# Condition vectors written as rows in eight pieces, and other order of small loads, in a two-block transformer kernel

## Chip, cores and metric

The kernel runs on one core of a Trainium2 chip. The metric is the device time of one execution in microseconds (us). TensorE is PE in the profile, VectorE DVE, ScalarE ACT, GpSimd POOL and SyncE SP; SP's queue issues nearly all transfers.

## What is computed

One sequence of 256 tokens of width 1024 goes through two blocks of two layers each. Block a has in each layer a gated feed-forward part (ffn), a mixer (retention, stick-breaking attention, state space) and a second ffn; block b has a mixer (three attentions) and an ffn. Every part is normalised, scaled and shifted by vectors that come from a condition `c`, and its result is gated by another such vector. Cut to one part of block a:

```python
mod = (silu(c) @ ada_w[l] + ada_b[l]).reshape(B, 9, 1024)[:, None]
u = modulate(rmsnorm(h, norm_ffn1[l]), mod[:, :, 0], mod[:, :, 1])   # u * (1 + scale) + shift
h = h + 0.5 * (1.0 + mod[:, :, 2]) * swiglu(u, ffn1_wg[l], ffn1_wu[l], ffn1_wd[l])
...
u = modulate(rmsnorm(h, norm_mix[l]), mod[:, :, 3], mod[:, :, 4])
...
h = h + (1.0 + mod[:, :, 5]) * mixed
```

All of it is in float32. There are 32 condition vectors of 1024 elements, each the product of the condition with 1024 x 1024 weights.

## The kernel before

**Work and stages.** The program is ten phases in a row: ffn, mixer, ffn for each layer of block a, then mixer, ffn for each layer of block b. The tokens are two tiles of 128 rows, `h[0]` and `h[1]`, which stay in SBUF. Every float32 product is three matmuls (`mm3`): each operand is split into a rounded high part H and a rest L, and H.H, H.L and L.H are added. A weight tile of 128 x 1024 is loaded by SP (`dma_next`, L306), cast to H by ACT (`prep_H`, L321), and DVE forms L = raw - H (`prep_L`, through `tt`, L185). The raw tiles, H, L, the condition tiles and the gate rows share one pool `s` of 36 buffers.

**An ffn.** For each block j of 256 hidden columns PE makes gate and up (`A`), ACT takes the silu (`post`, through `act`, L206), DVE multiplies (`m<-m,A`, L185), PE transposes the product (`trans`, through `tr`, L182, `T<-ident,m`), ACT and DVE split it into H and L, and `down` multiplies it into the accumulators `B`. Near a phase's end `ffn` yields event 0: `run` calls `fin_a(0)`, which adds the gated accumulators to `h[0]`, sums the squares on ACT, takes the reciprocal root on POOL (`rstd2`, L227 and L229), and normalises on DVE (`ts`, L198). Event 2 lets `fin_b(0)` transpose and modulate it for the next phase; event 1 does the second token tile.

**The condition vectors.** `ada_gen` runs beside the phases. For a vector it loads eight tiles of 128 x 1024 (`ada_load`, L501), and DVE multiplies each with the condition and sums (`ada_dot`, L506), one every `PACE[phase]` units of the program's own clock; a tile is asked for one dot ahead. The result is `v`, 128 x 8. Twenty of the vectors are used in this form. Twelve are gates (kinds h, p, c) and are needed as one row of 1024 on all partitions: `ada_fin` adds the bias on DVE (`g<-v,vtab`), ACT writes `v` as a row to DRAM (L550, `row<-g`), and ACT reads it back onto 128 partitions (L554, `s<-row`).

**Order.** Each engine takes its instructions in order. That order is made when the program is built: the phases' generator is the main lane, `ada_gen`, `ada_fin` and the weights' preparation are side lanes that are stepped whenever the main lane has advanced by so many units (`yield 3.0`, `self.pump(...)`), and a scheduler then places the instructions by their dependences and buffers. A DMA inside `issue_after(last_dma)` stays behind the load before it in SP's queue; one outside of it may be placed earlier. `d_skip` (L1272, the mixer of block a) and two gains `gqg` (L1373, the mixer of block b, from which POOL makes tables, L1377 and L1381) are loaded outside of it.

## Times and profile of the kernel before

| What | Value |
| --- | --- |
| median of three runs | 1949.09 us (1947.65 to 1954.33) |
| the profiled execution | 1949.93 us |
| its span | 1948.2 us |
| its mean granted clock of PE | 0.992 |
| PE busy | 1888.2 us, 97%, 9228 matmuls and transposes |
| DVE busy | 1452.8 us, 75% |
| ACT busy | 991.4 us, 51% |
| POOL busy | 68.7 us, 4% |

The span is the time from the first to the last instruction that the profile has. A busy time is the time in which the engine had an instruction at work. A timeline row gives start, duration, engine, line, operation, what it writes and reads, how many like it follow each other, and in brackets how long the engine had been idle just before and which instruction released it.

### The profile page before, as it was taken

The page shows a single profiled execution, that of the slowest core. Times are in us where ns is not written, and L with a number is a line of the kernel's source. Part 1 is how long each engine was busy: PE and PEld are TensorE (multiplying, and loading weights), DVE is VectorE, ACT ScalarE, POOL GpSimd, SP SyncE. Part 2 cuts the span into 40 slices and gives each one's busy share as a digit, 9 for nine tenths or more (in the row PEclk, how much of TensorE's full clock was granted, in tenths as well). Part 3 has the DMA queues.
Part 4 walks back from the last instruction along what each step waited for, and adds up shares of the span by engine and source line. Part 5 has one row for each costly group of instructions (what it writes and reads, how often), then busy time and mean ns, then how long its engine had stood idle before and what let it go on. Part 6 is the DMA issues. An engine that isn't in the chain of part 4 may idle for free.

```text
span 1948.2 us, 25535 instructions
## 1 busy us (share of the span) xinstructions
PE 1888.2 (97%) x9228; PEld 1555.2 (80%) x9228; DVE 1452.8 (75%) x2242; ACT 991.4 (51%) x1649; POOL 68.7 (4%) x135
## 2 busy tenths in 40 slices
PE   7999899999999999999989989999999899999998
PEld 5888798888888788988878868778888687778886
DVE  7877788788878786787777767678878576788552
ACT  5634556554445444576644435744544357546541
POOL 0000000100000000001000012100000011000000
PEclk9999999999999999999999999999999899999999
DMA  9979675389877896864698766467889663676650
GB/s 371 355 293 369 222 293 184 125 260 360 283 281 276 277 356 222 282 207 133 205 280 298 244 180 171 142 207 273 281 337 302 183 170 122 231 255 231 226 164 22
DMA packets 151344, 471.18 MB, mean 242 GB/s; under 512 B 36657, under 2 KB 36785, under 8 KB 151090
## 3 DMA queue, kind: packets, MB, share of 16 engines
q1 hardware_dynamic: 137010, 463.21, 69.2%
q10 hardware_dynamic: 14208, 6.34, 1.3%
q8 instruction: 72, 1.18, 0.2%
q14 instruction: 54, 0.44, 0.1%
HBM read 468.40 MB, written 1.10 MB: 241 GB/s over the span
## 4 chain that ended last, share of the span: by engine, by line
PE 59%; issue 28%; DVE 6%; DMA 4%; ACT 2%; POOL 1%; SPq 0%; ACTq 0%; DVEq 0%; POOLq 0%
PE A L170 39%; PE B L170 17%; PE T L182 3%; DVE s L185 2%; DMA row<-g 2%; DMA s<-in_ada_w 1%; DVE m L185 1%; ACT m L206 1%; ACT s L321 1%; DMA s<-in_ffn_wd 1%; DVE s L506 1%; DMA s<-in_ffn_gu 1%; DVE s L203 1%; DVE sm L1696 0%; DVE h L185 0%
## 5 line engine op out<-in xcount | busy, mean ns | idle before, releaser
L170 PE MATMUL A<-s,uH 128*128 128x512 f32 (+1 forms) x2976 | 936.2, 395 | 4.5 <-ACT uH L214 2.4
L185 DVE TENSOR_TENSOR s<-s,s 128x1024 fp32r<-128x1024 f32 (+2 forms) x638 | 754.1, 1198 | 124.7 <-ACT s L321 119.1
L321 ACT CAST s<-s 128x1024 fp32r<-128x1024 f32 (+1 forms) x618 | 624.0, 1043 | 96.7 <-DVE s L185 32.9
L170 PEld LDWEIGHTS A<-s,uH 128*128 128x128 f32 x2976 | 550.2, 189 | 121.7 <-issue 9.3
L170 PE MATMUL A<-s,uL 128*128 128x512 f32 (+1 forms) x1488 | 581.5, 392 | 0.3 <-DVE uL L185 0.3
L170 PE MATMUL B<-s,m 128*128 128x512 f32 (+2 forms) x1696 | 405.6, 387 | 0.7 <-ACT m L214 0.5
L170 PEld LDWEIGHTS B<-s,m 128*128 128x128 f32 x1696 | 310.6, 189 | 61.7 <-ACT m L214 1.9
L506 DVE SCALAR_TENSOR_TENSOR s<-s,cb 128x1024 f32<-128x1024 f32 x256 | 311.3, 1218 | 50.1 <-DMA s<-in_ada_w 43.5
L170 PEld LDWEIGHTS A<-s,uL 128*128 128x128 f32 x1488 | 280.4, 188 | 60.1 <-DVE uL L185 2.6
L206 ACT ACTIVATE m<-A 128x256 f32<-128x256 f32 x126 | 48.2, 383 | 246.6 <-PE A L170 246.4
L214 ACT CAST m<-T 128x256 fp32r<-128x256 f32 x132 | 48.9, 372 | 218.8 <-PE T L182 207.1
L170 PE MATMUL A<-uH,s 128*128 128x256 f32 (+1 forms) x672 | 128.0, 287 | 2.4 <-ACT s L1429 2.3
L185 DVE TENSOR_TENSOR m<-m,A 128x256 f32<-128x256 f32 x126 | 52.5, 417 | 86.0 <-ACT m L206 85.2
L182 PE MATMUL T<-ident,m 128*128 128x128 f32 (+1 forms) x488 | 85.6, 276 | 29.9 <-DVE m L185 27.7
L182 PEld LDWEIGHTS T<-ident,m 128*128 128x128 f32 (+1 forms) x488 | 62.8, 139 | 58.9 <-DVE m L185 33.1
L170 PEld LDWEIGHTS A<-uH,s 128*128 128x128 f32 (+1 forms) x672 | 105.6, 188 | 4.1 <-ACT s L1429 2.8
L170 PE MATMUL B<-s,s 128*128 128x512 f32 (+3 forms) x432 | 103.2, 384 | 0.9 <-ACT s L206 0.5
L185 DVE TENSOR_TENSOR m<-T,m 128x256 fp32r<-128x256 f32 x132 | 55.1, 420 | 56.8 <-ACT m L214 56.5
L170 PE MATMUL A<-uL,s 128*128 128x256 f32 (+1 forms) x336 | 95.5, 284 | 0.0
L170 PEld LDWEIGHTS B<-s,s 128*128 128x128 f32 (+1 forms) x432 | 78.7, 188 | 16.6 <-DVE s L203 1.3
L206 ACT ACTIVATE m<-h 128x512 f32<-128x512 f32 x44 | 27.8, 632 | 83.6 <-DVE h L185 83.6
L170 PEld LDWEIGHTS A<-uL,s 128*128 128x128 f32 (+1 forms) x336 | 63.3, 188 | 0.7
(189 smaller groups left out, 1193.6 us busy)
## 6 DMA issues: line engine op xcount, KB each, us to landing
s<-in_ffn_gu SPq DMA_DIRECT2D x264, 512.0 KB, 5.8
s<-in_ada_w SPq DMA_DIRECT2D x240, 512.0 KB, 6.5
s<-in_w_in_blk SPq DMA_DIRECT2D x152, 512.0 KB, 5.1
s<-in_ffn_wd SPq DMA_DIRECT2D x88, 512.0 KB, 5.8
s<-in_ffn_w_down SPq DMA_DIRECT2D x44, 512.0 KB, 4.8
s<-in_w_out SPq DMA_DIRECT2D x40, 512.0 KB, 4.3
s<-in_final_ada_w SPq DMA_DIRECT2D x16, 512.0 KB, 8.7
s<-row ACTq DMA_DIRECT2D x12, 512.0 KB, 7.3
```

The costliest lines, as they stand in the source:

```text
L170: self.last = self.nc.tensor.matmul(out, l, r, start=start, stop=stop, skip_group_check=True)
L182: self.nc.tensor.transpose(out, in_, self.ident[:p, :p])
L185: self.nc.vector.tensor_tensor(o, x, y, op=op)
L203: self.nc.vector.scalar_tensor_tensor(o, x, s, y, op0=op0, op1=op1)
L206: return self.nc.scalar.activation(o, x, f, **kw)
L214: self.nc.scalar.copy(H, x)
L321: self.last_H = self.nc.scalar.copy(H[:, :n], raw[:, :n])
L506: self.nc.vector.scalar_tensor_tensor(raw, raw, 1.0, self.cb, op0=ALU.mult, op1=ALU.mult, accum_out=v)
```

## The change

The vector v is transposed on PE to 8 x 128, copied by DVE, and written to DRAM as eight rows of 128; write and read are issued by SP, each with its place in the queue of loads. Condition tiles are asked for two dots ahead. The normalisation of the first token tile at the end of an ffn is put behind the last product (`post(j, 1)`, new event 3). The loads of `d_skip`, `gqg` and the constants keep their place in SP's queue (`queue`). Four of the ten paces differ. Lines below L405 move by up to 13.

```diff
--- before.py
+++ after.py
@@ -91,7 +91,7 @@
     return t.astype(np.float32)
 
 
-PACE = (3.2, 2.8, 4.1, 3.8, 3.6, 4.8, 4.8, 3.9, 5.0, 3.0)
+PACE = (3.9, 2.6, 4.1, 3.8, 3.6, 4.4, 3.6, 3.9, 5.0, 3.0)
 
 
 class Lane:
@@ -402,7 +402,7 @@
             evac(half, ps[:, :].rearrange("p (c n) -> p c n", c=2))
 
 
-    def fin_a(self, tt, accs, gate, extra=None):
+    def fin_a(self, tt, accs, gate, extra=None, lazy=False):
 
         h = self.h[tt]
         sq = self.m2([128, 512])
@@ -423,11 +423,15 @@
         r = self.rstd2(ss)
         if extra is not None:
             r = extra(tt, r)
-        xn = self.m4([128, 1024])
-        for nb in range(2):
-            c = slice(nb * 512, nb * 512 + 512)
-            self.ts(xn[:, c], h[:, c], r, ALU.mult)
-        return xn
+
+        def norm():
+            xn = self.m4([128, 1024])
+            for nb in range(2):
+                c = slice(nb * 512, nb * 512 + 512)
+                self.ts(xn[:, c], h[:, c], r, ALU.mult)
+            return xn
+
+        return norm if lazy else norm()
 
     def new_u(self):
         return (self.t([128, 2, 8, 128], "uH", 1, F32R), self.t([128, 2, 8, 128], "uL", 1, F32R))
@@ -496,6 +500,11 @@
         self.nc.sync.dma_start(self.cb, bass.AP(src.tensor, src.offset, [[0, 128], [1, 1024]]))
         self.act(self.cb, self.cb, AF.Silu)
 
+    def queue(self, out, in_):
+
+        with self.tc.issue_after(self.last_dma.ins):
+            self.last_dma = self.nc.sync.dma_start(out, in_)
+
     def ada_load(self, w, ft):
         raw = self.m4([128, 1024])
         self.nc.sync.dma_start(raw, w[ft * 128:ft * 128 + 128, :])
@@ -515,7 +524,8 @@
             ld.append(self.ada_load(items[i][1], ft))
 
         load(0)
-        yield 3.0
+        load(1)
+        yield 4.0
         for n, (i, ft) in enumerate(units):
             key, _, bias, cn, kind, gain = items[i]
             if cn != self.cb_of:
@@ -523,8 +533,8 @@
                 yield 8.0
             if ft == 0:
                 vs[i] = self.t([128, 8], "v8", 3)
-            if n + 1 < len(units):
-                load(n + 1)
+            if n + 2 < len(units):
+                load(n + 2)
             self.ada_dot(ld.pop(0), vs[i][:, ft:ft + 1])
             yield self.pace
             if ft == 7:
@@ -545,13 +555,17 @@
                 self.ts(v, v, 0.5, ALU.mult, 0.5, ALU.add)
             elif kind == "p":
                 self.ts(v, v, 1.0, ALU.add)
-            yield 2.5
+            yield 1.5
+            p = self.pT()
+            self.tr(p[:8, 0:128], v)
+            vt = self.t([8, 128], "vt", 1)
+            self.nc.vector.tensor_copy(vt, p[:8, 0:128])
+            yield 2.0
             d = self.t([8, 128], "row", 2, pool=self.dr)
-            self.nc.scalar.dma_start(d[:, :].rearrange("k p -> p k"), v)
-            yield 6.0
+            self.queue(d, vt)
+            yield 5.0
             g = self.m4([128, 1024])
-            row = d[:, :].rearrange("k p -> (k p)").unsqueeze(0)
-            self.nc.scalar.dma_start(g, row.to_broadcast([128, 1024]))
+            self.queue(g, d[:, :].rearrange("k p -> (k p)").unsqueeze(0).to_broadcast([128, 1024]))
             yield 4.0
             self.adv[key] = g
 
@@ -694,6 +708,7 @@
         yield 0, [acc[0, 0], acc[0, 1]]
         gu(b, 1, 2, 8, p, True)
         post(j, 1, p)
+        yield 3, None
         down(j - 1, 1, d, True)
         trans(j, 1)
         yield 2, None
@@ -742,11 +757,7 @@
         self.nones = self.t([128, 128], "nones", 1, pool=self.cst)
         nc.gpsimd.memset(self.nones, -1.0)
 
-        def table():
-            with self.tc.issue_after(self.last_dma.ins):
-                nc.sync.dma_start(self.ctab, a["ctab"])
-
-        self.later(60.0, table)
+        self.later(60.0, lambda: self.queue(self.ctab, a["ctab"]))
         self.filling = True
         self.fill_dma()
         self.ada = self.spawn([self.ada_gen(items[2:])], 4.0)
@@ -770,7 +781,9 @@
                     ex = self.final_mod if ph[i + 1][2][0][0] == "b" and ph[i][2][0][0] == "a" else None
                     if ex:
                         self.fm = self.fm if hasattr(self, "fm") else self.final_mod_prep()
-                    xn[ev] = self.fin_a(ev, accs, g["gate"], ex)
+                    xn[ev] = self.fin_a(ev, accs, g["gate"], ex, body == self.ffn and ev == 0)
+                elif ev == 3 and not last:
+                    xn[0] = xn[0]()
                 elif ev == 2 and not last:
                     nu = self.new_u()
                     g["G"], g["S"] = self.need(*ph[i + 1][2][0]), self.need(*ph[i + 1][2][1])
@@ -1269,7 +1282,7 @@
         yg = self.m4([128, 2, 512])
         dsk = self.t([128, 8], "dsk", 1)
         src = self.a["d_skip"][l:l + 1]
-        nc.sync.dma_start(dsk, bass.AP(src.tensor, src.offset, [[0, 128], [1, 8]]))
+        self.queue(dsk, bass.AP(src.tensor, src.offset, [[0, 128], [1, 8]]))
         for tt in range(2):
             self.mul(v8(yg[:, tt]), v8(xs[:, tt]), b8(dsk))
             self.add(yg[:, tt], yg[:, tt], Y[tt])
@@ -1370,7 +1383,7 @@
         for nm in ("gqa_q_norm_g_2", "gqa_k_norm_g_2"):
             g = self.t([128, 64], "gqg", 2)
             src = a[nm][l:l + 1]
-            nc.sync.dma_start(g, bass.AP(src.tensor, src.offset, [[0, 128], [1, 64]]))
+            self.queue(g, bass.AP(src.tensor, src.offset, [[0, 128], [1, 64]]))
             t = self.t([128, 2, 2, 64], "g1", 2)
             gs = g[:, :].rearrange("p (g s e) -> p g s e", g=2, s=2)
             for tt in range(2):
```

On DVE at the end of the first phase: `B` is an accumulator of the first token tile, `h_9` its residual, `s<-s,s` the L part of a weight tile, `m<-m,A` the last gated product, L198 the normalisation. Before:

```order
L185 TENSOR_TENSOR s_412_1662<-s_390_1568,s_411_1661 128x1024
L185 TENSOR_TENSOR h_9_76<-h_9_76,m_436_1790 128x512
L185 TENSOR_TENSOR m_437_1794<-B_761,s_280_1090 128x512
L506 SCALAR_TENSOR_TENSOR s_410_1655,v_365_1470<-s_410_1655,cb_116 128x1024
L185 TENSOR_TENSOR s_418_1693<-s_399_1616,s_417_1692 128x1024
L185 TENSOR_TENSOR h_9_76<-h_9_76,m_437_1794 128x512
L185 TENSOR_TENSOR s_422_1710<-s_403_1631,s_421_1709 128x1024
L185 TENSOR_TENSOR s_432_1771<-s_409_1650,s_431_1770 128x1024
L198 TENSOR_SCALAR s_440_1802<-h_9_76,sm_1800 128x512 x2
L185 TENSOR_TENSOR m_442_1825<-m_441_1823,A_1763 128x256
```

Now:

```order
L185 TENSOR_TENSOR s_415_1681<-s_395_1604,s_414_1680 128x1024
L185 TENSOR_TENSOR s_419_1698<-s_398_1616,s_418_1697 128x1024
L185 TENSOR_TENSOR m_434_1782<-B_760,s_290_1141 128x512
L185 TENSOR_TENSOR s_429_1759<-s_406_1639,s_428_1758 128x1024
L185 TENSOR_TENSOR h_9_76<-h_9_76,m_434_1782 128x512
L185 TENSOR_TENSOR m_438_1810<-m_437_1808,A_1751 128x256
L515 SCALAR_TENSOR_TENSOR s_413_1668,v_402_1628<-s_413_1668,cb_116 128x1024
L198 TENSOR_SCALAR s_439_1812<-h_9_76,sm_1788 128x512 x2
L185 TENSOR_TENSOR m_425_1745<-T_1827,m_424_1744 128x256
```

The product (`m<-m,A`) stood behind the normalisation, and now stands ahead of it and of a dot.

On ACT at the eleventh gate row, with the write L550, the broadcast read L554, weight casts (L321), a cast of a transpose (L214) and the silu (L206). Before:

```order
L550 DMA row_13760<-g_3099_13743 128x8x1
L214 CAST m_3086_13701<-T_13771 128x256
L321 CAST s_3102_13765<-s_3082_13687 128x1024
L321 CAST s_3106_13782<-s_3085_13699 128x1024
L206 ACTIVATE m_3112_13818<-A_13788 128x256
L554 DMA s_3111_13810<-row_13760 128x1024
L214 CAST m_3122_13850<-T_13852 128x256
```

Now, at the same place of the program (ACT has no transfer left there):

```order
L321 CAST s_3107_13738<-s_3082_13624 128x1024
L321 CAST s_3111_13752<-s_3086_13639 128x1024
L321 CAST s_3117_13771<-s_3092_13670 128x1024
L214 CAST m_3114_13758<-T_13825 128x256
L321 CAST s_3121_13786<-s_3096_13687 128x1024
L206 ACTIVATE m_3137_13870<-A_13842 128x256
L321 CAST s_3128_13819<-s_3109_13742 128x1024
```

On SP at the same gate row. Before, SP asked only for weights and condition tiles there:

```order
L306 DMA s_3082_13687<-in_ffn_w_down 128x1024
L306 DMA s_3085_13699<-in_ffn_w_down 128x1024
L306 DMA s_3091_13718<-in_ffn_w_down 128x1024
L501 DMA s_3093_13724<-in_ada_w 128x1024
L306 DMA s_3096_13734<-in_ffn_w_down 128x1024
L501 DMA s_3100_13757<-in_ada_w 128x1024
L306 DMA s_3104_13769<-in_w_in_blk 128x1024
L306 DMA s_3108_13786<-in_w_in_blk 128x1024
```

Now the write of the row and its read stand among them:

```order
L306 DMA s_3109_13742<-in_ffn_w_down 128x1024
L506 DMA row_13744<-vt_13719 8x128
L306 DMA s_3113_13756<-in_ffn_w_down 128x1024
L306 DMA s_3119_13775<-in_ffn_w_down 128x1024
L510 DMA s_3120_13780<-in_ada_w 128x1024
L306 DMA s_3123_13790<-in_ffn_w_down 128x1024
L506 DMA s_3126_13802<-row_13744 128x1024
```

Both transfers of the row have moved from ACT to SP; between them stand four loads.

## Rows read from the trace of the kernel before

**Rows 1.** The page, its part 1: busy time and share of the span.

```profile
PE 1888.2 (97%) x9228; PEld 1555.2 (80%) x9228; DVE 1452.8 (75%) x2242; ACT 991.4 (51%) x1649; POOL 68.7 (4%) x135
```

**Rows 2.** Timeline of PE: start us, us, instruction, count, [idle before <-releaser].

```profile
207.49 0.47 PE L182 MATMUL T<-ident,m 128*128 128x128 f32 x1 [5.34 <-DVE m L185]
...
680.68 0.33 PE L182 MATMUL T<-ident,m 128*128 128x128 f32 x1 [1.58 <-DVE m L185]
...
1001.51 0.48 PE L182 MATMUL T<-ident,m 128*128 128x128 f32 x1 [5.39 <-DVE m L185]
...
1113.86 0.33 PE L182 MATMUL T<-ident,m 128*128 128x128 f32 x1 [0.96 <-DVE m L185]
...
1133.38 0.33 PE L182 MATMUL T<-ident,m 128*128 128x128 f32 x1 [2.49 <-DVE m L185]
...
1528.14 0.47 PE L182 MATMUL T<-ident,m 128*128 128x128 f32 x1 [7.06 <-DVE m L185]
```

**Rows 3.** Stretches of PE: stretch, us, busy us (count), granted clock, DMA share, GB/s.

```profile
205.60:212.50 6.90, 4.79 (x16) 0.51 0.50 180
1001.00:1004.40 3.40, 2.89 (x8) 0.51 1.03 396
1134.10:1137.50 3.40, 3.40 (x9) 0.50 0.00 0
1528.20:1533.40 5.20, 5.20 (x14) 0.50 1.02 418
```

**Rows 4.** Timeline of ACT around the eleventh row write.

```profile
1502.79 0.41 ACTq L550 DMA_DIRECT2D row<-g  x1
...
1520.62 0.37 ACT L214 CAST m<-T 128x256 fp32r<-128x256 f32 x1 [11.61 <-DMA row<-g]
```

**Rows 5.** Timeline of DVE, same place.

```profile
1521.02 0.42 DVE L185 TENSOR_TENSOR m<-T,m 128x256 fp32r<-128x256 f32 x1 [10.34 <-ACT m L214]
...
1527.67 0.42 DVE L185 TENSOR_TENSOR m<-m,A 128x256 f32<-128x256 f32 x1
```

**Rows 6.** Waits of SP's queue: us in total, times, longest us.

```profile
SPq L306 <- DMA row<-g: 83.9, 9, 15.8
```

**Rows 7.** Timeline of SP in the seventh row write's time.

```profile
985.50 0.36 SPq L501 DMA_DIRECT2D s<-in_ada_w  x1
```

**Rows 8.** Timeline of DVE at two dots of condition tiles.

```profile
995.00 1.23 DVE L506 SCALAR_TENSOR_TENSOR s<-s,cb 128x1024 f32<-128x1024 f32 x1 [6.95 <-DMA s<-in_ada_w]
...
1131.76 1.22 DVE L506 SCALAR_TENSOR_TENSOR s<-s,cb 128x1024 f32<-128x1024 f32 x1 [2.14 <-DMA s<-in_ada_w]
```

**Rows 9.** Timeline of DVE at the end of the first phase.

```profile
197.20 0.69 DVE L185 TENSOR_TENSOR m<-B,s 128x512 f32<-128x512 f32 x1 [0.25 <-PE B L170]
197.81 1.22 DVE L185 TENSOR_TENSOR s<-s,s 128x1024 fp32r<-128x1024 f32 x1
198.94 0.68 DVE L185 TENSOR_TENSOR h<-h,m 128x512 f32<-128x512 f32 x1
...
206.23 0.88 DVE L198 TENSOR_SCALAR s<-h,sm 128x512 f32<-128x512 f32 x2 [0.77 <-POOL sm L229]
207.03 0.41 DVE L185 TENSOR_TENSOR m<-m,A 128x256 f32<-128x256 f32 x1
```

**Rows 10.** The transfers: issues, KB each, median us to landing.

```profile
row<-g ACTq DMA_DIRECT2D x12, 4.0 KB, 11.3
...
dsk<-in_d_skip SPq DMA_DIRECT2D x2, 4.0 KB, 2.9
```

**Rows 11.** Groups of PE by form: busy us, mean ns | idle before, releaser.

```profile
L182 PE MATMUL T<-ident,m 128*128 128x128 f32 x456 | 81.4, 276 | 29.9 <-DVE m L185 27.7 <-DVE m L198 1.9
```

**Rows 12.** POOL's table operations: ns min/median/max, first and last start.

```profile
L1381 POOL TENSOR_TENSOR g<-ctab,gqg x16: 241/251/1028, 879.6 to 1224.6; 128x32 f32<-128x32 f32 x16
...
L1377 POOL TENSOR_TENSOR g<-ctab,gqg x8: 310/322/2574, 879.4 to 1224.1; 128x64 f32<-128x64 f32 x8
```

**Rows 13.** Timeline of POOL at the first opening of the mixer of block b.

```profile
1162.53 0.30 POOL L227 TENSOR_SCALAR sm<-sm 128x1 f32<-128x1 f32 x1 [4.06 <-ACT m L206]
```

## The prediction

> **What bounds the kernel now.** I read the busy times first. TensorE (PE) is busy for 1888.2 of the span's 1948.2 us [rows 1], so its span is its own matmuls, some 60 us in which it stands, and the stretches in which its clock is at half. The change takes out no matmul and adds twelve small transposes. Whatever it gains must therefore come out of those 60 us and of the half-clock stretches.
>
> Then I read PE's timeline for its gaps. Apart from the prologue, six stand out, and all end with the same instruction, the transpose of a gated product (`T<-ident,m`, L182), which waits for DVE's product (L185): 5.34, 1.58, 5.39, 0.96, 2.49 and 7.06 us [rows 2]. In four places the granted clock is near 0.5 (1.2 GHz) behind such a wait [rows 3]; after the gaps of 1.58 and 0.96 us I find no such stretch. The question is what DVE was doing before each product.
>
> Behind the longest gap stands ACT. It issues the eleventh gate row's write at 1502.79 and does the next cast of a transpose at 1520.62, after 11.61 us that end with the landing of `row<-g` [rows 4]: the broadcast read (L554) is ACT's own instruction and must wait until the row lies in DRAM, and the casts queue behind it. DVE idles 10.34 us for that cast, then has a queue of casts and dots, and reaches the product only at 1527.67 [rows 5]. The row's landing takes 11.3 us at the median, 1024 pieces of four bytes; a load of the same 4 KB in other pieces (`dsk`) takes 2.9 [rows 10]. The gap of 1.58 us has the same pattern, smaller.
>
> Behind the gap of 5.39 us stands SP. Its weight loads waited for row writes for 83.9 us in nine waits [rows 6]. While the seventh row was being written SP stood still; the condition tile behind it was asked for at 985.50 only [rows 7], and DVE's dot stood 6.95 us for it, until 995.00, with the product behind it in its queue [rows 8]. The gap of 2.49 us follows a dot that waited 2.14 us [rows 8], again after a stop of SP at a row write; that of 0.96 is the tail of the same stop.
>
> Only the first gap, 5.34 us, has another cause: at the end of the first phase DVE does the last cast differences, then the normalisation, which waits for POOL (0.77 us), at 206.23, and the product behind it at 207.03 [rows 9].
>
> **The change part by part.** The sum is made against the profiled execution's 1949.9 us, which is 0.8 above the median of the three runs; I don't correct for that.
>
> *Gate rows as eight rows, on SP.* ACT no longer issues either transfer, so nothing of its casts waits for a row. A: the gap at 1528.14 goes (7.06), and with it the slow clock behind it: 5.20 us of PE at 0.50 would be 2.6 at full speed, so 2.6 more [rows 3]. Sum 9.7. B: the gap at 680.68, 1.6.
>
> The row is now 8 pieces of 512 bytes. No row shows this write; between 2.9 us (same bytes, `dsk`) and 11.3 (today) I take 2.9, since the number of pieces is what sets those two apart. SP asks for 0 to 4 loads between write and broadcast, where 5 to 13 lay between them, so it reaches the broadcast early and may stand there for up to a landing, twelve times. Behind it queue weight and condition loads, which the buffers cover: a stop of 3 us is shorter than the 83.9 / 9 = 9.3 us that SP stands at present. C: so the gap at 1001.51 goes: 5.39, and half of the 2.89 busy us at 0.51, 1.4; sum 6.8. D: the gaps of 0.96 and 2.49 with half of 3.40 at 0.50 would make 5.15 together, but the dots there also work close to their loads, so between 0 and 5.15 I take 3.0.
>
> Here a rule speaks against the change. By the rows, what held ACT was not the cost of issuing (0.41 us a write) but the landing. The Trainium skill, page "DMA: Bandwidth & Descriptors", section "Issuing engines are not separate DMA queues", says that DMAs run on the same 16 engines whichever engine starts them, so that another issuer saves only the time of starting. By that alone, moving 24 issues would give nothing on PE's path, and the sum would lose A and B unless the pieces themselves are quicker. The trace disagrees for ACT, whose waiting cost PE 7.06 us; but the rule makes the first rival below a serious one.
>
> *The transposes.* Twelve of them are new, in PE's own order. Each costs at most 0.276 us, the mean of a 128x128 one [rows 11]: 3.3 us, all on the path. Each also waits for its gate vector, the end of eight dots. The instruction order puts it 1 to 36 matmuls behind DVE's last operation on the vector, twice within two; bounds are 0 and 2.14 us each (a late tile, [rows 8]). I take 1.0 for all, nearest to 0 because ten have room. The copy of 8x128 on DVE and its operands lie beside PE's matmuls: nothing.
>
> *Two tiles ahead, and the new paces.* The dots keep nearly their places; a tile asked for one dot earlier has one more pace (about 4 us) to land. It is the second reason for C and D and is not counted again. It holds one more of 36 buffers; the weight loads' distances stay about the same in the order, so nothing.
>
> *Normalisation behind the last product.* E: the order shows that it is so at the first boundary alone; at the other ffn ends DVE's sequence is as before. From 197.20 on I replay the new sequence with the pitches of the old rows, 0.61 for an operation on 512 and 1.13 for a difference on 1024 [rows 9] and 1.2 for a dot: 0.61 + 1.21 + 0.61 + 1.13 + 1.13 + 0.61 + 1.13 + 0.61 = 7.04, so the product starts at 204.24 and the transpose at about 204.8 and not 207.49: 2.7 us sooner. The normalisation ends at about 207.1 as today, and four matmuls fill the time until its transposes. I count 2.7; bounds are 2.0 (the second wait is not all filled) and 7.8 (the gap goes and the slow clock, half of 4.79, with it).
>
> *Small loads keep their place.* `dsk` is asked for only about eleven matmuls before its use; with a landing of 2.9 us [rows 10] each of two places costs 0 to 2.9; I take 0.5 each, as the matmuls cover most of it. `gqg` now reaches POOL at both openings of the second mixer, and POOL makes twelve table operations ahead of the second token tile's reciprocal root: 4 x 0.322 + 8 x 0.251 = 3.3 us [rows 12], in an idle stretch of 4.06 [rows 13]. At their slowest (2.57 and 1.03 us once each) they overrun it. PE waits there already, so an overrun counts: 0 to some 2.3 us; I take 0.5.
>
> The sum: gains 9.7 + 1.6 + 6.8 + 3.0 + 2.7 = 23.8; costs 3.3 + 1.0 + 1.0 + 0.5 = 5.8. Net 18.0: 1949.9 - 18.0 = 1932, about 0.9% faster.
>
> **The rivals.** *The wait moves with the issue.* If the row still takes about 11 us to land, because it shares the way with the 512 KB tiles that are under way, SP stands at twelve broadcasts for 8 us or more, and the tiles behind it come late as now. For it: SP already stops for row writes [rows 6]. Against it: `dsk`, also 4 KB, lands in 2.9 us among the same tiles. Then C and D stay, and A, B and E give 14.0 less the 5.8 of costs: 1949.9 - 8.2 = 1941.7. The rule quoted above would have it so.
>
> *The gaps only move.* DVE is 75% busy [rows 1] and nearly all waits end at its products; where ACT and SP no longer hold it, its own queue of differences and dots could be what is late next, with small gaps at other products. For it: E itself is such a queue. Against it: in the long gaps DVE was idle first (10.34 and 6.95 us [rows 5, 8]). If three quarters of the gain return, 1949.9 - 23.8 / 4 + 5.8 = 1949.8: no change.
>
> *Slower: PE stands at the new transposes.* Before, a late condition tile held up a product somewhere down DVE's queue; now its vector has a transpose in PE's own order, and nothing on PE passes it. If each of the twelve stood as long as the dot at 1131.76 did, 2.14 us [rows 8], that is 25.7 us: 1949.9 - 18.0 + 25.7 - 1.0 (already counted) = 1956.6. It decides from (18.0 + 1.0) / 12 = 1.6 us each on, and is told from no change at 2.1 each. Against it: ten of twelve have matmuls between, and tiles are asked for earlier.
>
> *The change does less than it says.* The postponed normalisation moves only at one boundary; if that too only shifts the wait to the next transposes, E goes: 1934.6, inside the forecast's range.
>
> **How the numbers follow.** Forecast 0.72; the wait moves with the issue 0.13; gaps only move 0.08; slower 0.07. A measurement of this kernel tells a difference from none at about 0.3%, 5.8 us, so faster means under 1943.2 and slower over 1954.9. 1941.7 lies just on the faster side: of its 0.13, 0.11 count as faster and 0.02 as same. Faster 0.83, same 0.10, slower 0.07. With all bounds at their best (D 5.15, E 7.8, nothing but the 3.3 against them) the net is 31.05 - 3.3 = 27.8, 1922; with D and E at their worst and `dsk` and POOL at half of theirs it is 20.1 - 8.4 = 11.7, 1938. The range takes in the first rival and a little below the best sum, for small gaps that I have not counted: 1920 to 1944.
>
> **What would show it.** Right: no wait of ACT for `row<-g`, a landing near 3 us, SP's waits for rows well under half of 83.9, PE's gaps at 680, 1001 and 1528 gone with their slow clock, and one near 2.6 us at 202. Wrong: landings near 10 us (first rival), PE waits at `T<-ident,g` that sum to more than 5 us (slower), `T<-ident,m` gaps of the old total at new places (gaps move), or a PE wait of over 2 us at the transposes of the second token tile where block b's mixer opens, behind POOL's tables.

## The result, and the profile after

The changed kernel takes 1922.59 us (median of four runs, 1922.02 to 1923.49) where the kernel before takes 1948.37 beside it: a ratio of 0.9863, 95% interval 0.9841 to 0.9885, so 1.4% faster, about 26 us. 1932 had been forecast, with a range of 1920 to 1944. The direction and the range held; the gain was half as large again as the sum of 18.

The experiments below ran on other chips, where the kernel before took 1955 to 1957; they are compared by their ratio, or by their span against that of the changed kernel. On two of those three chips the changed kernel's own sequence of instructions ran beside them (experiments 6 and 9), at a ratio of 0.984.

The page of the changed kernel, part 1 ([rows 1] for the kernel before):

```profile
span 1921.7 us, 25594 instructions
## 1 busy us (share of the span) xinstructions
PE 1884.8 (98%) x9240; PEld 1554.0 (81%) x9240; DVE 1455.0 (76%) x2254; ACT 988.6 (51%) x1649; POOL 66.5 (3%) x135
```

PE's busy time fell by 3.4 us although twelve instructions came in; the rest of the 26.5 us of span is idle time that has gone (from 60.0 to 36.9 us). Its waits for the gated products, and DVE's for condition tiles, from the list of waits of the changed kernel (us in total, times, longest):

```profile
PE T L182 <- DVE m L185: 6.8, 7, 1.7
...
DVE s L515 <- DMA s<-in_ada_w: 3.4, 5, 1.8
```

Before:

```profile
PE T L182 <- DVE m L185: 28.0, 14, 7.1
...
DVE s L506 <- DMA s<-in_ada_w: 43.5, 25, 7.0
```

SP's own waits for the two steps of a row:

```profile
SPq L506 <- DVE vt L562: 40.8, 9, 11.0
...
SPq L506 <- DMA row<-vt: 10.8, 4, 5.1
```

SP stood 83.9 us for rows in its weight loads alone [rows 6]; now 10.8 in all. A new wait has come in that I had not forecast: SP stands 40.8 us for the copy of the transposed vector, because the row write has its place among the loads. The loads behind it bear that: DVE's waits for condition tiles have shrunk to 3.4 us all the same.

To find where the time came from I take the start of the same instruction in both traces, the first transpose of a normalised tile at the end of each phase, in us from the start of the span. At the end of phase 1 four `B` matmuls have moved ahead of it, so there the two are not quite at the same place.

| End of phase | before | changed | saved so far |
| --- | --- | --- | --- |
| 1, ffn (a) | 207.97 | 202.81 | 5.2 |
| 2, mixer (a) | 390.88 | 384.34 | 6.5 |
| 3, ffn (a) | 577.91 | 571.81 | 6.1 |
| 4, ffn (a) | 767.77 | 759.73 | 8.0 |
| 5, mixer (a) | 946.92 | 939.21 | 7.7 |
| 6, ffn (a) | 1148.29 | 1129.00 | 19.3 |
| 7, mixer (b) | 1350.85 | 1334.68 | 16.2 |
| 8, ffn (b) | 1549.09 | 1522.41 | 26.7 |
| 9, mixer (b) | 1747.86 | 1722.18 | 25.7 |
| span | 1948.2 | 1921.7 | 26.5 |

Four steps carry the gain: 6.5 in the first two phases, 1.9 in the fourth, 11.6 in the sixth, 10.5 in the eighth. The seventh gives 3.1 back. Timeline rows of PE in the changed kernel, at what is left ([rows 2] for before):

```profile
200.24 0.44 PE L182 MATMUL T<-ident,m 128*128 128x128 f32 x2 [1.73 <-DVE m L185]
...
1127.19 0.44 PE L182 MATMUL T<-ident,m 128*128 128x128 f32 x2 [0.70 <-DVE m L185]
1129.00 0.52 PE L182 MATMUL T<-ident,s 128*128 128x128 f32 x3 [1.37 <-DVE s L198]
...
1315.50 0.72 PE L170 MATMUL B<-s,s 128*128 128x512 f32 x2 [1.71 <-DVE s L203]
```

The transpose that waited 5.34 us waits 1.73; the gaps of 1.58, 5.39, 0.96, 2.49 and 7.06 us have no successor over 0.25 us. The row at 1127.19 is the transpose after the one that waited 2.49; before, it waited 0.17:

```profile
1146.47 0.44 PE L182 MATMUL T<-ident,m 128*128 128x128 f32 x2 [0.17 <-DVE m L185]
```

The wait of 1.37 us behind it stood there before as well. The last row is a new gap, in the mixer of block b. The granted clock still falls behind some of them (stretch, us, PE busy, granted clock, DMA share, GB/s):

```profile
201.80:205.20 3.40, 3.29 (x13) 0.50 0.88 300
1130.20:1133.60 3.40, 3.17 (x11) 0.50 0.48 31
1171.20:1174.60 3.40, 3.18 (x15) 0.50 0.55 166
1560.30:1563.70 3.40, 3.40 (x16) 0.50 0.66 189
```

At 1171 and in the first phase there was such a stretch before as well. That of 1134 to 1137.5 [rows 3] has another in its place at 1130, so in this execution the saving of D's slow clock did not last past the sixth phase's end, and the one at 1560 is new.

### The profile page after: what moved, and what is told of

The parts are those of the page before. It is cut to its first block, busy times and chain, and to the rows that moved or that the text cites. A ratio compares the mean times of both kernels' runs of the same rounds, so it can differ in the third digit from the quotient of the medians.

```text
span 1921.7 us, 25594 instructions
## 1 busy us (share of the span) xinstructions
PE 1884.8 (98%) x9240; PEld 1554.0 (81%) x9240; DVE 1455.0 (76%) x2254; ACT 988.6 (51%) x1649; POOL 66.5 (3%) x135
## 4 chain that ended last, share of the span: by engine, by line
PE 65%; issue 27%; DVE 4%; ACT 1%; POOL 1%; DMA 1%; SPq 0%; DVEq 0%; POOLq 0%; ACTq 0%
PE A L170 42%; PE B L170 19%; PE T L182 3%; DVE s L185 2%; DVE m L185 1%; DMA s<-in_ada_w 1%; PE T L170 1%; ACT m L206 0%; ACT s L321 0%; DVE s L515 0%; POOL sm L229 0%; POOL sm L221 0%; DVE h L185 0%; DVE m L203 0%; DVE s L203 0%
## 5 line engine op out<-in xcount | busy, mean ns | idle before, releaser
L321 ACT CAST s<-s 128x1024 fp32r<-128x1024 f32 (+1 forms) x618 | 621.9, 1043 | 47.9 <-DVE s L185 28.7
L206 ACT ACTIVATE m<-A 128x256 f32<-128x256 f32 x126 | 48.3, 383 | 287.1 <-PE A L170 286.9
L214 ACT CAST m<-T 128x256 fp32r<-128x256 f32 x132 | 48.8, 372 | 205.7 <-PE T L182 205.7
L206 ACT ACTIVATE m<-h 128x512 f32<-128x512 f32 x44 | 27.8, 632 | 84.3 <-DVE h L185 84.3
```

The lines of the kernel that those rows point to most:

```text
L206: return self.nc.scalar.activation(o, x, f, **kw)
L214: self.nc.scalar.copy(H, x)
L321: self.last_H = self.nc.scalar.copy(H[:, :n], raw[:, :n])
```

## Experiments

**1. Eight rows, but issued by ACT.** The kernel before with one edit:

```diff
-            yield 2.5
+            yield 1.5
+            p = self.pT()
+            self.tr(p[:8, 0:128], v)
+            vt = self.t([8, 128], "vt", 1)
+            self.nc.vector.tensor_copy(vt, p[:8, 0:128])
+            yield 2.0
             d = self.t([8, 128], "row", 2, pool=self.dr)
-            self.nc.scalar.dma_start(d[:, :].rearrange("k p -> p k"), v)
-            yield 6.0
+            self.nc.scalar.dma_start(d, vt)
+            yield 5.0
```

Expected:

> The kernel before with one edit: the vector is transposed and written as eight rows of 512 bytes, but ACT still issues the write and the broadcast read. Theory (the pieces: it was the landing of 1024 four-byte pieces that held ACT and SP): the row lands in 3 us or less, ACT no longer stands for it, the gaps of 7.06 (with its slow clock), 1.58, 5.39 and 0.96 + 2.49 us go, twelve transposes cost 3.3: 1948.4 - 21 + 3.3 = about 1930. Rival (the issuer: what counts is that ACT does not issue): ACT still stands at the broadcast, its gap stays, over 1940.

Measured: 1928.74 us, ratio 0.9859 (0.9837 to 0.9881), span 1925.3. ACT's waits for a row, where the kernel before had waits up to 11.61 us [rows 4], are down to one:

```profile
ACT s L321 <- DMA row<-vt: 0.8, 1, 0.8
```

The gaps of 1.58, 5.39, 2.49 and 7.06 us are gone, that of 0.96 is 0.41, and the first phase's end still has one of 5.13. By the table's landmarks phase 6 gives 11.2 us and phase 8 9.6, as in the changed kernel. So nearly all of C, D and A comes from the form of the write; who issues it does not matter once the row lands soon. SP's loads still stood for the rows that ACT issued, 19.8 us in seven waits, where it was 94.3 in eleven before; why a load of SP waits for a write that ACT issued, no run shows.

**2. The pieces again, issued by SP.** The changed kernel, with the row written from `v`, 128 x 8, in the queue of loads:

```diff
-            yield 1.5
-            p = self.pT()
...
-            yield 2.0
+            yield 2.5
             d = self.t([8, 128], "row", 2, pool=self.dr)
-            self.queue(d, vt)
-            yield 5.0
+            self.queue(d[:, :].rearrange("k p -> p k"), v)
+            yield 6.0
```

Expected:

> The changed kernel with one part undone: the row is written from the 128 x 8 vector in 1024 four-byte pieces again, without transposes, but by SP, in the queue of loads. Theory (the pieces): SP stands about 8 us at most of twelve broadcasts, condition tiles and weights come late as before, the gaps behind DVE's dots (5.39, 0.96, 2.49) come back in some form, less 3.3 for the transposes: about 1930. Rival (the issuer): the loads are covered by their buffers, and without the transposes it is 1919 to 1923.

Measured: 1937.05 us, ratio 0.9897 (0.9879 to 0.9916), span 1936.3, 14.6 us longer than the changed kernel's. SP's waits, its timeline at the ninth row, DVE's first wait behind it, and PE's gap:

```profile
SPq L506 <- DMA row<-g: 81.1, 12, 10.8
```

```profile
1112.58 0.43 SPq L506 DMA_DIRECT2D row<-g  x1
1123.87 0.33 SPq L506 DMA_DIRECT2D s<-row  x1
1124.77 0.38 SPq L1748 DMA_DIRECT2D s<-in_final_norm  x1
```

```profile
1131.57 1.23 DVE L203 SCALAR_TENSOR_TENSOR s<-s,s 128x1024 f32<-128x1024 f32 x1 [8.55 <-DMA s<-in_final_norm]
```

```profile
1140.95 0.47 PE L182 MATMUL T<-ident,m 128*128 128x128 f32 x1 [7.89 <-DVE m L185]
```

SP writes the row at 1112.58 and stands until 1123.87 for its landing; the load of `final_norm` behind it is asked for at 1124.77, DVE waits 8.55 us for it, and PE 7.89 for the product behind that in DVE's queue. This is the first rival of the prediction in the flesh: the wait moves with the issue. It stood 6.8 us a row (81.1 / 12; I had put 8 or more), and the load that came late here is another than the condition tiles that I had in mind. Two row writes earlier it went the same way: a gap of 3.82 us at 855 and a slow clock behind it, by which phase 5 lost 6.6 us against the kernel before. The gap that stood at 1528 does not come back (phase 8 still gives 11.0), because ACT has no part in the row any more. So either half of the change, fewer pieces or another issuer, would have freed ACT; only fewer pieces free SP.

**3. Tiles asked for two ahead, alone.** The kernel before, with `load(1)` after `load(0)`, `yield 4.0` and `load(n + 2)`. Expected:

> The kernel before with one edit: condition tiles are asked for two dots ahead. Theory (the pieces): ACT stands for rows as before, so the 7.06 us gap stays; of the gaps behind late condition tiles (5.39, 0.96, 2.49 us) some go: 1940 to 1948. Rival (the loads ahead are what gives the gain at 1000 and 1130): those gaps are gone entirely, SP's stops cost nothing, 1937 to 1940.

Measured: 1952.55 us, ratio 0.9983 (0.9966 to 0.9999), span 1947.9, so at best 0.3% faster. SP's waits and the longest one of DVE:

```profile
SPq L306 <- DMA row<-g: 80.7, 9, 15.3
```

```profile
1110.89 1.23 DVE L506 SCALAR_TENSOR_TENSOR s<-s,cb 128x1024 f32<-128x1024 f32 x1 [9.74 <-DMA s<-in_ada_w]
```

```profile
1118.64 0.48 PE L182 MATMUL T<-ident,m 128*128 128x128 f32 x1 [6.64 <-DVE m L185]
```

SP stands for rows as before (the total of 83.9 has become 80.7), and a tile asked for earlier still cannot be asked for while SP stands: the wait of DVE is even longer, and PE has a gap of 6.64 us behind it. The rival falls. The theory holds for SP and not for ACT: ACT stands for a row only once, for 2.2 us, and the gap of 3.86 us that comes after the eleventh row in place of the 7.06 follows a late condition tile. At the first phase's end the product stands ahead of the normalisation (208.96 and 213.43) although nothing postpones it in this kernel, and PE's gap there is 5.73 us all the same. "A second reason for C and D", which the prediction gave the two tiles ahead, has no support here.

**4. The rows' part alone.** The kernel before with the eight rows and `queue` for both transfers of the row, nothing else. Expected:

> The kernel before with the gate rows' part of the change alone: eight rows, written and read back by SP in its queue. Theory (the pieces): nearly the whole gain of the change except the 2.7 to 6 us at the first phase's end: 1925 to 1930. If the loads ahead, the paces and the postponed normalisation do much beside it, it is above 1933; the issuer's rival gives the same here as the theory.

Measured: 1928.86 us, ratio 0.9858 (0.9837 to 0.9879), span 1930.7. Against experiment 1 only the issuer and its place in the queue differ, and the medians by 0.1 us; the spans of the two profiled executions differ by 5.4, and 4.8 of that lies before the end of phase 2, most of it in the prologue, ahead of any row (a gap of 2.88 us with a slow clock behind it, against 1.64 without). The profiled execution is the slowest of its four, whose spans go from 1925.4 to 1930.7, so that difference may be this execution's alone. Beside the 0.984 of the changed kernel on two other chips, the rows' part gives most of the gain, some nine tenths; the table's landmarks put what is missing into the first two phases, where this execution falls 3.4 us behind the kernel before and the changed kernel has saved 6.5.

**5. Tiles one ahead.** The changed kernel with the loads of the kernel before. Expected:

> The changed kernel with condition tiles asked for one dot ahead again. Theory (the rows' pieces made SP late, and that is mended by itself): 0 to 2 us above the changed kernel's 1922.6, so 1922 to 1925. Rival (asking earlier is what took away the gaps behind late condition tiles): waits of DVE for condition tiles of 2 us and more, with gaps of PE behind them, 1928 to 1932.

Measured: 1926.28 us, ratio 0.9854 (0.9837 to 0.987), span 1923.4. DVE's waits for condition tiles rise from 3.4 to 8.1 us in all, the longest 2.1. Up to phase 6 the kernel is even 1.5 us ahead of the changed one; then it loses that and more to a gap in the mixer of block b, at the same instruction as the changed kernel's 1.71:

```profile
1314.29 0.50 PE L170 MATMUL B<-s,s 128*128 128x512 f32 x1 [3.29 <-DVE s L203]
```

The theory holds: with rows that land soon, asking earlier is worth some 2 us (1.7 by the spans; 2.0 by the medians of this run and of the next, which stands for the changed kernel on this chip). That is a balance of gains and losses and not a property of the earlier loads alone: with one ahead the first phase ends 2.2 us sooner, the second loses 1.3 of that, and with the old pace in the mixer of block b one ahead is not the slower (experiments 11 and 12).

**6. The normalisation where it was.** The changed kernel with `lazy` always `False`. Expected:

> The changed kernel with the normalisation ahead of the last product again. Theory (the replay of DVE's queue): the gap at the first phase's end, 1.73 us in the changed kernel, grows to about 4.5 to 5.5 and nothing else changes: 1925 to 1927. Rival (the wait only shifts from one transpose to the next, so the move is worth nothing): within 1 us of 1922.6.

Measured: 1924.27 us, ratio 0.984 (0.9826 to 0.9855), span 1923.0, the gap at the first phase's end 1.74 us: the same as the changed kernel. Theory and rival both assumed that the order differs. It does not: with the names' numbers left out, each of the five engines has the same rows in the same order in both kernels. The scheduler puts the normalisation behind the product with or without the postponement. As the two are one sequence of instructions, the 1.3 us between their spans is no effect (the executions of experiment 9 span 1921.7 to 1924.9 us, all of one kernel), and this run is the measure for the other three of its chip.

**7. The ten old paces.** Expected:

> The changed kernel with the ten old paces of the dots. Theory (the paces are a fine setting): within 2 us of 1922.6, and the new gap of 1.71 us in the first mixer of block b, where the new pace puts more dots, is gone. Rival (the paces carry part of the gain in the first phase, which ended 5.2 us earlier in the changed kernel): first phase 2 us or more longer, 1925 to 1928.

Measured: 1927.21 us, ratio 0.9857 (0.9842 to 0.9872), span 1925.8, so 2.9 us over experiment 6 by the medians and 4.1 over the changed kernel by the spans. The gap at the first phase's end is 5.97 us, and the one of 1.71 in the mixer of block b is gone. The rival holds for the first phase: 4.3 us are lost by the end of phase 2; what phase 6 loses besides, phase 7 gives back.

**8. The small loads free.** The changed kernel where `d_skip` and the two gains are plain DMAs again. Expected:

> The changed kernel where the loads of d_skip and of the two gains do not keep their place in the queue, as in the kernel before. Theory: three small loads stand in SP's queue at the program's start again, and a gap of 1.6 to 3 us at 27 us comes back that the kernel before and three of four experiments show and the changed kernel does not: 1924 to 1927. Rival (the loads in place cost what I had put down for them, 1.5 us, and gain nothing): 1920 to 1922.

Measured: 1927.58 us, ratio 0.9856 (0.9841 to 0.9871), span 1926.3: 3.3 us over experiment 6 by the medians, 4.6 over the changed kernel by the spans. SP's first loads here, and PE's gap and clock behind them:

```profile
14.08 0.33 SPq L1285 DMA_DIRECT2D dsk<-in_d_skip  x1
15.33 0.33 SPq L1386 DMA_DIRECT2D gqg<-in_gqa_q_norm_g  x1
16.57 0.33 SPq L1386 DMA_DIRECT2D gqg<-in_gqa_k_norm_g  x1
17.84 1.57 SPq L510 DMA_DIRECT2D s<-in_ada_w  x2
```

```profile
28.10 1.23 DVE L515 SCALAR_TENSOR_TENSOR s<-s,cb 128x1024 f32<-128x1024 f32 x1 [4.02 <-DMA s<-in_ada_w]
```

```profile
30.86 0.50 PE L170 MATMUL B<-s,uH 128*128 128x512 f32 x1 [3.26 <-DVE s L185]
```

```profile
31.40:34.80 3.40, 3.40 (x9) 0.50 1.03 422
```

Loads leave SP about 1.25 us apart at that time, small ones too (14.08, 15.33, 16.57). With three of them ahead the next condition tile is asked for at 17.84, and at 13.23 in the changed kernel, whose loads began 0.85 us sooner. DVE waits 4.02 us for a tile, PE 3.26, and the clock is halved for 3.4 us. The theory holds. The kernel before has the same three loads at 13.06, 14.30 and 15.52.

**9. The changed kernel again,** as the measure of the next three. Expected:

> The changed kernel itself once more, on the chip of the three variants beside it, as their measure. Both theories: 0.985 to 0.987 of the kernel before, its span within 1 us of 1921.7.

Measured: 1924.56 us (1923.48 to 1926.73), ratio 0.984 (0.9819 to 0.9861), span 1921.7.

**10. The first phase's pace alone back at 3.2.** Expected:

> The changed kernel with the pace of the first phase alone back at 3.2. Theory (the gap at the first phase's end is set by how many dots and differences stand in DVE's queue, that is by the pace, not by the normalisation's place): the gap of 1.73 us becomes about 6, as with all old paces, and the span is 3.5 to 4.5 us longer. Rival (one of the other three paces did it): within 1 us of the repeated changed kernel.

Measured: 1928.90 us, ratio 0.9862 (0.9842 to 0.9882), span 1927.1, 5.4 us longer. DVE's queue at the first phase's end, PE's gap, and the stretch of slow clock:

```profile
197.75 0.69 DVE L185 TENSOR_TENSOR m<-B,s 128x512 f32<-128x512 f32 x1 [1.41 <-PE B L170]
198.36 1.22 DVE L185 TENSOR_TENSOR s<-s,s 128x1024 fp32r<-128x1024 f32 x1
199.49 0.69 DVE L185 TENSOR_TENSOR h<-h,m 128x512 f32<-128x512 f32 x1
200.09 1.22 DVE L185 TENSOR_TENSOR s<-s,s 128x1024 fp32r<-128x1024 f32 x1
201.23 1.22 DVE L515 SCALAR_TENSOR_TENSOR s<-s,cb 128x1024 f32<-128x1024 f32 x1
202.37 0.08 DVE L515 DVE_READ_ACCUMULATOR s<-s,cb 128x1 f32 x1
202.37 0.69 DVE L185 TENSOR_TENSOR m<-B,s 128x512 f32<-128x512 f32 x1
202.98 1.22 DVE L185 TENSOR_TENSOR s<-s,s 128x1024 fp32r<-128x1024 f32 x1
204.11 0.69 DVE L185 TENSOR_TENSOR h<-h,m 128x512 f32<-128x512 f32 x1
204.71 0.41 DVE L185 TENSOR_TENSOR m<-m,A 128x256 f32<-128x256 f32 x1
```

```profile
205.27 0.45 PE L182 MATMUL T<-ident,m 128*128 128x128 f32 x1 [5.97 <-DVE m L185]
```

```profile
201.40:211.60 10.20, 5.39 (x15) 0.50 0.52 181
```

From 197.75 to the product at 204.71 DVE works without a pause, 6.96 us, which is what the same stretch takes in the changed kernel (192.82 to 199.78). Here too the product stands ahead of the normalisation (209.19). So neither the normalisation's place nor the length of the stretch differs, but its start: DVE idles 1.41 us at 197.75 until PE has the accumulator `B`. PE's own order has changed with the pace. In the changed kernel twelve `B` matmuls stand ahead of the last nine `A` matmuls, here 24 stand behind all of them; first two rows of the changed kernel, then one of this run:

```profile
190.83 2.93 PE L170 MATMUL B<-s,m 128*128 128x512 f32 x12
...
192.82 0.68 DVE L185 TENSOR_TENSOR m<-B,s 128x512 f32<-128x512 f32 x1
```

```profile
193.70 5.60 PE L170 MATMUL B<-s,m 128*128 128x512 f32 x24
```

The pace of 3.2 puts 48 dots ahead of the product, the new one 43; PE needs the product at 199.30 here and at 198.51 in the changed kernel. The slow clock lasts 10.2 us here. The theory holds for the pace; that dots standing in DVE's queue there make the gap, as it had it, the idle time before 197.75 speaks against. The loss is 5.4 us (4.3 by the medians) in place of 3.5 to 4.5.

**11. The mixer's pace alone back at 4.8.** Expected:

> The changed kernel with the pace of block b's first mixer alone back at 4.8. Theory (the changed pace put dots ahead of DVE's L203 there and made the new gap of 1.71 us at 1314): that gap goes, 1 to 2 us faster than the repeated changed kernel, if the dots that are moved on to the next phase do no harm. Rival (the dots only move: an equal wait in the next phase): same as the changed kernel or up to 2 us slower.

Measured: 1923.76 us, ratio 0.9835 (0.9815 to 0.9855), span 1922.4. The gap of 1.71 us is gone, as the theory has it; by the end of phase 7 the kernel is 1.8 us ahead of experiment 9 (3.1 ahead of the changed kernel of the table, which had the slow clock at 1130 that experiment 9 has not). In phase 8, which starts with three gaps of 0.3 to 0.7 us, 2.3 are lost again. Whether it is faster at all stays unclear.

**12. One tile ahead, and the mixer's pace at 4.8.** Expected:

> Meant to be better than both: the changed kernel with tiles asked for one dot ahead, and the pace of block b's first mixer back at 4.8. With one ahead alone the first 1146 us took 2.5 us less than in the changed kernel, and a gap of 3.29 us with a slow clock behind it in that mixer took it back. Theory: that gap goes, 2 to 3 us faster than the repeated changed kernel. Rival (with one ahead the mixer's late product has another cause): the gap stays, same as the changed kernel or slower.

Measured: 1923.02 us (1921.42 to 1923.46), ratio 0.983 (0.9809 to 0.985), span 1919.6; the gap of 3.29 us is gone. All five of its runs lie below all four of the repeated changed kernel, by 1.5 us in the median, but the intervals of the ratios overlap widely: it is the fastest here, and faster than the kernel before, but than the changed kernel by too little to be sure.

## Why the prediction held, and where it was wrong

**A and B** (9.7 and 1.6): right in cause and size. Phase 8 saved 10.5 and phase 4 1.9; experiment 1, where ACT still issues, saved 9.6 and 1.4, so it is the landing that ACT stood for.

**C and D** (6.8, and 3.0 of at most 5.15): right in cause, D too small. (The row of C is the eighth, which the prediction called the seventh.) Phase 6 saved 11.6, close to the sum of both upper ends, 11.95. With tiles asked for one ahead it saved 11.9 (experiment 5), so the two tiles ahead are no second reason for it. Part of it, the slow clock, was given back at the start of the mixer.

**How long the row takes.** I took 2.9 us for the write of eight pieces. The list of transfers has no landing for it, but SP's four waits for a row end with one. The longest of the four, 5.1 us, and a short one, 1.3 us:

```profile
434.75 0.29 SPq L506 DMA_DIRECT2D row<-vt  x1
440.66 0.33 SPq L506 DMA_DIRECT2D s<-row  x1
...
1109.32 0.29 SPq L506 DMA_DIRECT2D row<-vt  x1
1111.00 0.34 SPq L506 DMA_DIRECT2D s<-row  x1
```

So the row took 5.9 us in one place and 1.7 in the other; in the two between it took some 4.7 and 5.0. My 2.9 was too small for three of the four; it cost little, as the write holds SP for 10.8 us in all.

**The first rival and the rule.** It needed a row that still lands in some 11 us. With that put back (experiment 2) SP did stand and the tiles behind did come late. The section "Issuing engines are not separate DMA queues" (Trainium skill, "DMA: Bandwidth & Descriptors") says that another issuer saves only the time that it takes to start the transfer. For the transfers these runs agree: experiments 1 and 4 differ in the issuer, and by 0.1 us of median. For the engine that must wait they show more than that: which engine stands for the landing decides whose work comes late (ACT's casts at 1520 before, SP's loads at 1124 in experiment 2).

**The transposes** (3.3, and 1.0 of waits): mis-sized. I used the duration of a row that ends a stretch [rows 11], where the path sees only how far the next instruction is pushed back:

```profile
1106.88 0.27 PE L182 MATMUL T<-ident,g 128*8 128x128 f32 x1
1106.90 0.70 PE L170 MATMUL A<-s,uH 128*128 128x512 f32 x2
1107.45 0.40 PE L170 MATMUL A<-s,uL 128*128 128x512 f32 x1
1107.68 0.62 PE L170 MATMUL A<-s,uH 128*128 128x512 f32 x2
```

From the transpose at 1106.88 to the third matmul at 1107.45 it is 0.57 us, in which two matmuls start; two take 0.46 at the pitch of 0.23 from 1107.45 to 1107.68. That leaves 0.11 us for the transpose, and 1.3 for twelve. None of the twelve has idle time ahead of it. The rival "slower", which lived on such waits, found none.

**E** (2.7): the gain is there, its cause was another. The step that failed is "Normalisation behind the last product": I read the new order beside the old and put its difference down to the part of the change that names it. Experiment 6 shows that this part moves nothing, and experiments 3 and 10 that the order alone does not help: both have the product ahead of the normalisation, and gaps of 5.73 and 5.97 us. What does is the pace of the first phase (experiment 10): with it PE finishes the accumulator earlier in its order, and DVE's sequence starts earlier. The length of my replay was right (7.04 us; 6.96 in the changed kernel and in experiment 10), but in the changed kernel the sequence starts 4.4 us earlier than the 197.20 that I had it start at. That a gain came at this place all the same (the gap fell from 5.34 to 1.73 us) is luck.

**Small loads** (costs 1.0 + 0.5): wrong in sign. "Apart from the prologue, six stand out" passed over a gap of 2.96 us at 29.52, which the change touches (and others of 1.4 to 1.7 us further on): three of the loads that I priced at their new places stood in the prologue's queue. Putting them behind is worth 3.3 to 4.6 us (experiment 8). At their new places no wait of DVE for `d_skip` appears. POOL's tables took 4.64 us and not 3.3, and the second tile's reciprocal root follows them without a pause, 5.64 us after the first one's, where it was 5.09 before: about the 0.5 us that I had put; PE's gap there is 1.39 us, 1.41 before.

**The first two phases as a whole.** By the end of phase 2 the changed kernel has saved 6.5 us. Without the new pace it is 0.0 (experiment 10; 2.2 with all ten old paces, experiment 7), without the moved loads 0.5 (experiment 8, where a slow clock at 31.4, worth some 1.7, comes in that the kernel before has not). Each part is worth little there alone: with the old pace PE stands 5.97 us at the phase's end, and with the loads in the prologue the time is lost at the start. I had also put the two tiles ahead at nothing: a gap of 1.65 us at 307.71 is 0.43 in the changed kernel, 0.48 or less in all the others that ask two ahead, and 1.65 to 2.19 in all that ask one ahead.

**The sum.** By the table phases 1 and 2, 4, 6 and 8 gave 30.5 us where A to E had 23.8; more than half of the difference, 3.8, lies in the first two, and 1.8 in phase 6. The other phases gave back 4.0, where the costs were put at 5.8; 3.1 of the 4.0 went in phase 7, at a slow clock and a gap that I had not forecast. The net is 26.5 in place of 18.0.

**The other rivals.** "The gaps only move" came true in small: 1.71 us in the mixer of block b and the slow stretch at 1560. "Less than it says" came true for the normalisation: its postponement is worth nothing, and the gain at that place came from other parts.

What stays open: why the pace changes PE's order, which the program's scheduler makes; how long the eight-piece write takes in the eight places where SP did not wait for it; and which of the paces and distances is best: the last two experiments move 1 to 2 us from phase to phase.

## What to carry to other kernels

Look for the transfer made of many tiny pieces even when its bytes are nothing: 12 x 4 KB held up ACT or SP here, and changing its form was worth some 1.4% alone, while moving it to another queue as it was (experiment 2, with all other parts of the change) moved the wait to what that queue carries, and left 1.0%. When a change has several parts, undo each one, and compare the engines' orders first: one part here moved no instruction at all, and two parts were worth 6.5 us together and 0 to 2 apart. Price an added PE instruction by how far it pushes the next one, and look at the prologue's gaps too when a change moves loads that may be issued there.

## What the runs showed of the hardware that I had not expected

- Near the start, loads leave SP 1.25 us apart, and a load of 4 KB takes the same slot as one of 512 KB (experiment 8).
- A transpose of 128 x 8 lists 0.27 us but pushes the next matmul back by 0.11.
- PE's clock did not always fall after a like wait: after 2.96 us idle at 29.52 the kernel before stayed at 1.00, after 3.26 experiment 8 fell to 0.50 for 3.4 us. In the changed kernel two waits of 0.70 and 1.37 us close together were followed by 3.4 us at 0.50; in experiment 9, the same sequence of instructions, waits of 0.78 and 1.38 us there were not. A saved gap can therefore be worth its length and some 1.7 us more (half of 3.4 us at 0.50), or not.
